# One input block beside each group of routing weights, 24 routed slots in that stage, weights read back for eight blocks at a time

## The chip, the cores and the metric

The kernel runs on one core of a Trainium2 chip. The metric is device time in microseconds, from launch to the last output; the times shown are medians over a few executions, and one execution was also recorded by the hardware profiler.

## The reference

One layer of a diffusion backbone over 512 tokens of width 1024. An adaLN, a mixer made of three head groups and an output projection come first; the change leaves them alone. Then comes an expert layer (PEER) with 16384 experts, of which each token uses 128:

```
q = (t @ w_q).reshape(n_tok, PEER_HEADS, 2, PEER_QDIM // 2)
s = einsum('thid,hikd->thik', q, sub_keys)      # 8 heads, 2 halves, 128 keys
v1, i1 = top_k(s[:, :, 0], 16);  v2, i2 = top_k(s[:, :, 1], 16)
top_s, pos = top_k(v1[..., :, None] + v2[..., None, :], 16)   # 16 experts a head
idx = i1 * 128 + i2 at pos;  g = softmax(top_s)               # 128 experts a token
act = gelu(einsum('tkd,td->tk', u_tab[idx], t))
out = einsum('tk,tkd->td', g * act, v_tab[idx])
return rmsnorm(h + g2 * out, final_g)
```

## The kernel before

**Two ways through the expert layer.** The tokens are four tiles of 128. Tiles 0 to 2 (384 tokens) go densely: the 16384 experts are 128 blocks of 128. For each block `a` TensorE multiplies the block of `u_tab` with the tokens (`u_block`: 24 matmuls with 384 columns, three for each of 8 chunks, because every fp32 operand is split into a high and a low part, `wh` and `wl`; the text calls it a U block). ScalarE applies GELU, the result is multiplied by the block's routing weights (`e_w`), split again (`wwh`, `wwl`), and multiplied with the block of `v_tab` (`e_v`: 18 matmuls of 512 columns, three into each of six PSUM accumulators; a V block). Tile 3 (128 tokens) goes by gathers, one of its 128 routed slots `k` after the other: `g_load` gathers one row of 8 KB for each token (POOL), `g_dot` forms the dot product (VectorE, DVE), `g_act` applies GELU and the gate (ScalarE, ACT: `actG`, `wG`), `g_acc` adds to `accG` (DVE).

**Stages.** After scores and top-k comes `weights_T`, which turns the routing into a dense table of weights. It runs over 3 tiles of 16 steps `q8`, here 48 groups. In a group DVE builds two one-hot operands (`oi`, `ow`), TensorE multiplies them (16 small matmuls into `gdps`, which take the high part of `ow` first and the low part second), and ACT copies the result out in two pieces (`stg`). Each four groups fill one `stg`, which is written to DRAM (`gd_d`, 2 MB). Blocks of the list `AHEAD` are taken through `u_block` and GELU early and their result is kept in DRAM (`act_d`): the generator `ahead_steps` does one of them at each `next(ahead)`. In `weights_T` that is in the groups of `UQ`, 12 of each 16. A slot of tile 3 is spread over four groups there: `g_acc(k - 1)`, `g_load(k + 3)` and `g_dot(k)` in the first, `g_act(k)` in the second.

**The loop over blocks.** Then the loop `for i in range(-6, P + 1)` takes the 128 blocks: V block `i`, the U block of `i + 2` unless it is in `AHEAD` (then `act_d` is read back as `acl`), and the slots `kG[i]` to `kG[i + 1]` of tile 3. The loads run on SP's queue in the order in which the loop calls `e_load` and `e_weights`; a load waits there for a free buffer, and what stands behind it on SP waits too.

The order of the instructions on each engine is that of the code (`manual_schedule`); every engine works its list in order.

Of the kernel before, what the change touches and what calls it, by code (L numbers as in the profile page):

```python
# [7 lines left out]
F32 = mybir.dt.float32  # L8
# [4 lines left out]
AF = mybir.ActivationFunctionType  # L13
ALU = mybir.AluOpType
# [3 lines left out]
P = 128  # L18
D = 1024
# [4 lines left out]
NX = SEQ // P  # L24
# [8 lines left out]
TQ = 32  # L33
NQ = TD // TQ
# [109 lines left out]
    "cst": (P, NCST), "pcnt": (P, 4 * SEQ),  # L144
}

NAHEAD = 74
AHEAD = [a for a in range(128) if a * NAHEAD % 128 < NAHEAD]


def build(tc, A, out, dbg=None):
# [1370 lines left out]
    def g_load(k):  # L1522
        if k < P:
            rows[k] = gt.tile([P, 2 * D], F32, name="row")
            G.indirect_dma_start(out=rows[k], out_offset=None, in_=A["peer_uv"],  # L1525
                                 in_offset=bass.IndirectOffsetOnAxis(ap=idxG[:, k:k + 1], axis=0))
# [9 lines left out]
    def g_acc(k):  # L1536
        row = rows.pop(k)
        if k:
            V.scalar_tensor_tensor(accG, row[:, D:2 * D], wG[:, k:k + 1], accG, ALU.mult, ALU.add)  # L1539
        else:  # L1540
            V.tensor_scalar(accG, row[:, D:2 * D], wG[:, k:k + 1], None, ALU.mult)
# [14 lines left out]
        V.scalar_tensor_tensor(gwT[:, qs, 1, :], by8(2), GSCALE, gwT[:, qs, 0, :], ALU.mult, ALU.subtract)  # L1556

    gq = {}

    def weights_T(t):  # L1560
        for q8 in range(16):
            if q8 % 4 == 0:
                stg = sg.tile([P, P, TQ], F32, name="stg")

            def tb(ap):
                return ap[:, t * 16 + q8].rearrange("p w (g c) -> p (w g) c", c=2).unsqueeze(2).broadcast_to([P, 8, P, 2])
            oi = gs2.tile([P, 2, 4, P, 2], F16, name="oi", bufs=3)
            V.tensor_tensor(oi.rearrange("p w g b c -> p (w g) b c"), iotaA.unsqueeze(1).broadcast_to([P, 8, P, 2]), tb(ixT), ALU.is_equal)
            ob, oa = oi[:, 0], oi[:, 1]
            ow = gs2.tile([P, 2, 4, P, 2], F16, name="ow", bufs=3)  # L1570
            for w in range(2):
                V.tensor_tensor(ow[:, w], oa, tb(gwT)[:, w * 4:w * 4 + 4], ALU.mult)
            oh, ol = ow[:, 0], ow[:, 1]
            for q4 in range(2):
                ps = psD.tile([P, 4, P], F32, name="gdps")
                for j in range(4):
                    tt = q4 * 4 + j
                    pr, c = tt // 2, tt % 2
                    PE.matmul(ps[:, j, :], ob[:, pr, :, c], oh[:, pr, :, c], start=True, stop=False)
                    PE.matmul(ps[:, j, :], ob[:, pr, :, c], ol[:, pr, :, c], start=False, stop=True)  # L1580
                t0 = q8 % 4 * 8 + q4 * 4
                S.activation(stg[:, :, t0:t0 + 4].rearrange("p a t -> p t a"), ps, AF.Copy, scale=1.0 / GSCALE)  # L1582
            if q8 % 4 == 3:
                (nc.gpsimd if t == 2 and q8 == 15 else nc.scalar).dma_start(gd_d[t * 4 + q8 // 4], stg)
            if q8 in UQ:
                next(ahead, None)
            k = t * 4 + q8 // 4
            gq[0] = stg
            if q8 % 4 == 0:
                if k:  # L1590
                    g_acc(k - 1)
                    g_load(k + 3)
                g_dot(k)
            elif q8 % 4 == 1:
                g_act(k)

    UQ = (0, 1, 3, 4, 5, 7, 8, 9, 11, 12, 13, 15)

    def whole(gen):
        for _ in gen:  # L1600
# [26 lines left out]
    psD = gdp.ps("psD", bufs=4)  # L1627
    for t in range(3):
        weights_T(t)
    g_acc(11)  # L1630
    g_load(15)
    whole(ahead)


# [4 lines left out]
    esp = Pools()  # L1639
    ex = esp.sb("ex", bufs=2)  # L1640
    glp = Pools()
    gl = glp.sb("gl", bufs=3)
    gls = [gl]
    psV = ep.ps("psV", bufs=1)
    accT = [[psV.tile([P, 512], F32, name=f"pv{t}{hf}") for hf in range(2)] for t in range(3)]
# [20 lines left out]

    def e_weights(a):

        if a % 4 == 0:
            n = NQ if a else NQ - 1  # L1670
            gd = gds[a // 4] = gls[a // 4 % 2].tile([P, NQ, 4 * TQ], F32, name="gd", bufs=1)
            nc.sync.dma_start(gd[:, 0:n, :], gd_d[0:n, :, a:a + 4, :].rearrange("q b a t -> b q (a t)"))
            if n < NQ:
                G.tensor_copy(gd[:, n, :], gq[0][:, 0:4, :].rearrange("p a t -> p (a t)"))

    def e_u(a):
        if a in AHEAD:
# [5 lines left out]
    def e_w(a):  # L1683

        x = ac.pop(a)
        xq = x.rearrange("p (q t) -> p q t", q=NQ)
        V.tensor_tensor(xq, xq, gds[a // 4][:, :, a % 4 * TQ:(a % 4 + 1) * TQ], ALU.mult)  # L1687
        wh = ex.tile([P, TD], F32R, name="wwh", bufs=3)
        wl = ex.tile([P, TD], F32R, name="wwl", bufs=3)
        lows[a, 2] = []  # L1690
        split(wh, wl, x, None, lows[a, 2])
        ww[a] = (wh, wl)
# [8 lines left out]
    def f_load():  # L1701

        nc.sync.dma_start(fgr, A["rowg"][:, D:2 * D])
        for t in (3, 0, 1, 2):
            nc.sync.dma_start(hx[:, t, :], h_d[t * P:(t + 1) * P, :])
        row_bc(g2r, psu, 2, 2)

    def f_mul(t, hf):

        if hf == 0:  # L1710
            sqs[t] = gt.tile([P, 2 * D], F32, name="row")
            fss[t] = e1.tile([P, 2], F32, name="fss", bufs=2)
        sq = sqs[t]
        hs = slice(hf * 512, (hf + 1) * 512)
        src = accT[t][hf] if t < 3 else accG[:, hs]
        if "peer" in dbg:
            V.tensor_copy(sq[:, hs], src)
            nc.sync.dma_start(dbg["peer"][t * P:(t + 1) * P, hs], sq[:, hs])
        V.tensor_tensor(sq[:, hs], src, g2r[:, hs], ALU.mult)
        (V if t == 2 else G).tensor_tensor(hx[:, t, hs], sq[:, hs], hx[:, t, hs], ALU.add)  # L1720

    def f_sq(t, hf):
        hs = slice(hf * 512, (hf + 1) * 512)
        S.activation(sqs[t][:, hs], hx[:, t, hs], AF.Square, accum_out=fss[t][:, hf:hf + 1])

    def f_rstd(t):
        V.tensor_tensor(fss[t][:, 0:1], fss[t][:, 0:1], fss[t][:, 1:2], ALU.add)
# [1 line left out]

    def f_gain(t, hf):  # L1730
        hs = slice(hf * 512, (hf + 1) * 512)
        (V if t == 2 else G).tensor_tensor(sqs[t][:, D + hf * 512:D + hf * 512 + 512], hx[:, t, hs], fgr[:, hs], ALU.mult)

    def f_norm(t):
        r = f_rstd(t)
# [11 lines left out]
    def within(f, i):  # L1747
        if 0 <= i < P:
            f(i)
    LAST = 3  # L1750
    kG = [12 + min(P - 12, (i * (P - 12) + 120) // 121) for i in range(P + 1)]
    with order:
        e_weights(0)
        sgp.close()
        gls.append(glp.sb("gl2"))
        e1 = ep.sb("e1", side="right")
        g2r = e1.tile([P, D], F32, name="g2r")
        fgr = e1.tile([P, D], F32, name="fgr")
        hx = e1.tile([P, NX, D], F32, name="hx")
        for i in range(-6, P + 1):  # L1760
            within(lambda a: e_load(a, 0), i + 6)
            within(lambda a: e_load(a, 1), i + 4)
            if i > -5:
                within(e_weights, i + 5)
            now = range(kG[i], kG[i + 1]) if 0 <= i < P else ()
            within(e_w, i + 1)
            for k in now:
                g_dot(k)
            within(lambda a: e_high(a, 0), i + 3)
            within(lambda a: e_high(a, 1), i + 1)  # L1770
            within(lambda a: e_low(a, 2), i + 1)
            within(lambda a: e_low(a, 0), i + 3)
            within(lambda a: e_low(a, 1), i + 1)
            for k in now:
                g_act(k)
            within(e_u, i + 2)
            for k in now:
                g_acc(k)
                g_load(k + 4)
            if 0 <= i < P - LAST:  # L1780
                for t in range(3):
                    e_v(i, t)
                del ww[i]
            if i == 64:
                f_load()
            if i == P - 4:
                f_mul(3, 0)
                f_mul(3, 1)
            if i == P - 3:
                f_sq(3, 0)  # L1790
                f_sq(3, 1)
                f_gain(3, 0)
                f_gain(3, 1)
            if i == P - 1:
# [50 lines left out]
```

## Time and profile before

| | before |
|---|---|
| median of 3 executions | 1920.64 us (1919.88 to 1920.69) |
| the profiled execution, its own time | 1921.22 us |
| its span, first to last instruction | 1919.5 us |
| TensorE (PE) busy | 1833.6 us, 96% |
| VectorE (DVE) busy | 1397.4 us, 73% |
| ScalarE (ACT) busy | 829.5 us, 43% |
| GpSimd (POOL) busy | 413.8 us, 22% |
| mean granted TensorE clock | 0.986 |

A record of a matmul runs from its start to a modelled end, and neighbours overlap; rates are read from start to start. In a row of the timeline, the bracket at the end gives the idle time just ahead of the instruction and what ended it.

### The profile page before, as it was taken

The numbers are of one execution on the slowest core, as the hardware profiler recorded it, in microseconds if no ns is written. First come the engines' busy times: TensorE is split into PE (matmuls) and PEld (weight loads), VectorE is DVE, ScalarE is ACT, GpSimd is POOL, SyncE is SP. The second block draws the span as 40 slices with busy tenths as digits, with TensorE's granted clock in tenths as the row PEclk, the third lists the DMA queues.
The fourth block names the chain that finished last, engine by engine and source line by source line (L and its number), as shares of the span: only waits on it lengthen the run. The fifth ranks groups of instructions, "written<-read, shape, count | busy, mean of one in ns | idle before, by whom it ended". The sixth has DMA issues, their size and how long they took to land.

```text
span 1919.5 us, 26340 instructions
## 1 busy us (share of the span) xinstructions
PE 1833.6 (96%) x9703; PEld 1543.0 (80%) x9703; DVE 1397.4 (73%) x2682; ACT 829.5 (43%) x1491; POOL 413.8 (22%) x309
## 2 busy tenths in 40 slices
PE   6999998878999899999899999999999999999997
PEld 4687776655777788999888988888888888888886
DVE  5553149996642458988788878878878778878875
ACT  4332224414643433345666754434444444444443
POOL 1102226572002554330001011111111111111103
PEclk9999999988999999999999999999999999999999
DMA  9546231216422443356578779998999998999971
GB/s 357 163 140 200 79 131 55 67 39 226 143 66 77 134 139 109 113 176 247 213 288 303 289 290 392 351 365 324 351 353 328 374 384 321 366 339 333 367 254 65
DMA packets 210194, 446.75 MB, mean 233 GB/s; under 512 B 13424, under 2 KB 137072, under 8 KB 192112
## 3 DMA queue, kind: packets, MB, share of 16 engines
q1 hardware_dynamic: 172192, 259.25, 40.4%
q0 software_dynamic: 18576, 136.32, 18.2%
q10 hardware_dynamic: 19296, 49.49, 7.1%
q8 instruction: 76, 1.25, 0.3%
q14 instruction: 54, 0.44, 0.1%
HBM read 394.81 MB, written 52.30 MB: 233 GB/s over the span
## 4 chain that ended last, share of the span: by engine, by line
PE 78%; DVE 11%; ACT 6%; issue 3%; DMA 1%; ACTq 0%; POOL 0%; SPq 0%; DVEq 0%; POOLq 0%
PE pv L188 9%; PE pv L187 9%; PE pv L189 9%; PE pu L187 8%; PE pu L189 8%; PE pu L188 8%; PE acc L187 4%; PE acc L188 4%; PE acc L189 4%; ACT stg L1582 2%; PE acc L419 1%; DVE wl L180 1%; PE acc L421 1%; PE po L1049 1%; PE acc L423 1%
## 5 line engine op out<-in xcount | busy, mean ns | idle before, releaser
L180 DVE TENSOR_TENSOR wl<-wraw,wh 128x1024 fp32r<-128x1024 f32 x290 | 357.3, 1248 | 164.5 <-ACT wh L177 160.6
L177 ACT ACTIVATE wh<-wraw 128x1024 fp32r<-128x1024 f32 x324 | 335.9, 1052 | 223.7 <-PE acc L188 75.1
L187 PE MATMUL pu<-u2h,wh 128*128 128x384 f32 (+2 forms) x1040 | 355.1, 341 | 0.2 <-ACT g2r L1093 0.2
L189 PE MATMUL pu<-u2h,wl 128*128 128x384 f32 (+2 forms) x1040 | 351.0, 338 | 2.5 <-DVE wl L180 2.5
L188 PE MATMUL pu<-u2l,wh 128*128 128x384 f32 (+2 forms) x1040 | 350.9, 337 | 0.0
L1525 POOL DMA_INDIRECT row<-in_peer_uv,idxG x128 | 134.6, 1051 | 849.0 <-DVE accG L1539 742.9
L188 PE MATMUL pv<-wl,wwh 128*128 128x512 f32 x768 | 303.2, 395 | 0.0
L187 PE MATMUL pv<-wh,wwh 128*128 128x512 f32 x768 | 303.1, 395 | 0.0
L189 PE MATMUL pv<-wh,wwl 128*128 128x512 f32 x768 | 303.1, 395 | 0.0
L187 PEld LDWEIGHTS pu<-u2h,wh 128*128 128x128 f32 x1040 | 197.1, 189 | 3.4 <-ACT g2r L1093 1.0
L189 PEld LDWEIGHTS pu<-u2h,wl 128*128 128x128 f32 x1040 | 196.9, 189 | 2.9 <-DVE wl L180 2.9
L188 PEld LDWEIGHTS pu<-u2l,wh 128*128 128x128 f32 x1040 | 196.9, 189 | 2.3
L189 PEld LDWEIGHTS pv<-wh,wwl 128*128 128x128 f32 x768 | 144.4, 188 | 34.4
L188 PEld LDWEIGHTS pv<-wl,wwh 128*128 128x128 f32 x768 | 144.4, 188 | 32.1 <-DVE wl L180 0.2
L187 PEld LDWEIGHTS pv<-wh,wwh 128*128 128x128 f32 x768 | 144.3, 188 | 32.1
L1539 DVE SCALAR_TENSOR_TENSOR accG<-row,wG,accG 128x1024 f32<-128x1024 f32 x127 | 162.4, 1279 | 0.0
L1530 DVE CUSTOM_DVE_ANT_0 row<-row,u2G 128x1024 f32<-128x1024 f32 x128 | 156.0, 1219 | 0.0
L1687 DVE TENSOR_TENSOR act<-act,gd 128x384 f32<-128x384 f32 x54 | 31.3, 579 | 131.3 <-ACT act L1681 130.5
L177 ACT ACTIVATE wwh<-acl 128x384 fp32r<-128x384 f32 x74 | 38.9, 526 | 191.7 <-DVE acl L1687 169.0
L1681 ACT ACTIVATE act<-pu 128x384 f32<-128x384 f32 x54 | 26.5, 491 | 207.3 <-PE pu L189 207.3
L1582 ACT ACTIVATE stg<-gdps 128x512 f32<-128x512 f32 x96 | 98.1, 1163 | 26.0 <-PE gdps L1580 21.6
L180 POOL TENSOR_TENSOR wl<-wraw,wh 128x1024 fp32r<-128x1024 f32 x34 | 81.7, 2404 | 113.2 <-ACT wh L177 94.7
(412 smaller groups left out, 3249.7 us busy)
## 6 DMA issues: line engine op xcount, KB each, us to landing
wraw<-in_peer_ut SPq DMA_DIRECT2D x128, 512.0 KB
wraw<-in_peer_uv SPq DMA_DIRECT2D x128, 512.0 KB
gd<-gd_d SPq DMA_DIRECT2D x31, 768.0 KB
gd_d<-stg ACTq DMA_DIRECT2D x11, 2048.0 KB
wraw<-in_w_in SPq DMA_DIRECT2D x36, 512.0 KB
acl<-act_d SPq DMA_DIRECT2D x74, 192.0 KB
act_d<-act ACTq DMA_DIRECT2D x72, 192.0 KB
kT<-in_ada_w SPq DMA_DIRECT2D x18, 512.0 KB
```

Of the source, the lines that this page charges most:

```text
L177: S.activation(hi, full, AF.Copy)
L180: (eng or V).tensor_tensor(lo, full, hi.bitcast(F32), ALU.subtract)
L187: PE.matmul(ps, ah, bh, start=start, stop=False)
L188: PE.matmul(ps, ah, bl, start=False, stop=False)
L189: PE.matmul(ps, al, bh, start=False, stop=stop)
L419: PE.matmul(px, h[:, k, :], uh[:, k, :], start=s, stop=False)
L1525: G.indirect_dma_start(out=rows[k], out_offset=None, in_=A["peer_uv"], in_offset=bass.IndirectOffsetOnAxis(ap=idxG[:, k:k + 1], axis=0))
L1530: V.tensor_tensor_reduce(row[:, 0:D], row[:, 0:D], u2G, 1.0, 0.0, ALU.mult, ALU.add, actG[:, k:k + 1])
L1539: V.scalar_tensor_tensor(accG, row[:, D:2 * D], wG[:, k:k + 1], accG, ALU.mult, ALU.add)
L1582: S.activation(stg[:, :, t0:t0 + 4].rearrange("p a t -> p t a"), ps, AF.Copy, scale=1.0 / GSCALE)
L1681: S.activation(ac[a], pu[:, :TD], AF.Gelu)
L1687: V.tensor_tensor(xq, xq, gds[a // 4][:, :, a % 4 * TQ:(a % 4 + 1) * TQ], ALU.mult)
```

## The change

It does six things. `NAHEAD` goes from 74 to 86, so 86 blocks are in `AHEAD` and 42 are not. Each of the 48 groups of `weights_T` gets a `next(ahead)`, where 36 had one. A slot of tile 3 is spread over two groups and not four (`k = t * 8 + q8 // 2`), so 24 slots stand there and not 12; `g_act` stands in every odd group. In the loop, the weights are read back for eight blocks in one load (four for the first and the last), one iteration earlier, and `acl` has four buffers for three. The slots that are left are dealt to the iterations in proportion to 1 for an iteration without and 2 for one with a U block. The residual rows `hx` are loaded at `i == P - 6` and not at `i == 64`, into a buffer of the weights and into `u2G`.

```diff
-NAHEAD = 74
+NAHEAD = 86
 def weights_T(t):
...
-            if q8 in UQ:
-                next(ahead, None)
-            k = t * 4 + q8 // 4
+            next(ahead, None)
+            k = t * 8 + q8 // 2
             gq[0] = stg
-            if q8 % 4 == 0:
+            if q8 % 2 == 0:
                 if k:
                     g_acc(k - 1)
                     g_load(k + 3)
                 g_dot(k)
-            elif q8 % 4 == 1:
+            else:
                 g_act(k)
-    UQ = (0, 1, 3, 4, 5, 7, 8, 9, 11, 12, 13, 15)
...
-    g_acc(11)
-    g_load(15)
+    g_acc(NMID - 1)
+    g_load(NMID + 3)
     whole(ahead)
...
-    gl = glp.sb("gl", bufs=3)
+    gl = glp.sb("gl", bufs=4)
...
     def e_weights(a):
-        if a % 4 == 0:
+        if a % 8 == 4 or a == 0:
+            m = 8 if 0 < a < P - 4 else 4
...
-            nc.sync.dma_start(gd[:, 0:n, :], gd_d[0:n, :, a:a + 4, :].rearrange("q b a t -> b q (a t)"))
+            nc.sync.dma_start(gd[:, 0:n, :], gd_d[0:n, :, a:a + m, :].rearrange("q b a t -> b q (a t)"))
...
-    kG = [12 + min(P - 12, (i * (P - 12) + 120) // 121) for i in range(P + 1)]
+    done = [sum(1 if a + 2 in AHEAD else 2 for a in range(i)) for i in range(P + 1)]
+    kG = [NMID + min(P - NMID, -(-done[i] * (P - NMID) // done[P - 8])) for i in range(P + 1)]
...
-                within(e_weights, i + 5)
+                within(e_weights, i + 6)
...
             if i == 64:
                 f_load()
+            if i == P - 6:
+                h_load()
```

The order on DVE in the middle of `weights_T`, one slot of tile 3 with the groups around it. `wl` is the low part of a U block to come, the two ISA rows are `g_dot`, `oi` and `ow` belong to a group of routing weights. Before, over four groups:

```order
L180 TENSOR_TENSOR wl<-wraw,wh 128x1024 [waits DMAHW5_49,Activation_49]
L1539 SCALAR_TENSOR_TENSOR accG<-row,wG,accG 128x1024
L1530 ISA row,actG<-row,u2G 128x1024 [waits DMASW2_49]
L1530 ISA actG 128x1
L1568 TENSOR_TENSOR oi<-iotaA,ixT 128x2048 [waits PE_49]
L1572 TENSOR_TENSOR ow<-oi,gwT 128x1024 [waits DVE_49]
L1572 TENSOR_TENSOR ow<-oi,gwT 128x1024
```

Of the change, over two groups:

```order
L180 TENSOR_TENSOR wl<-wraw,wh 128x1024 [waits DMAHW5_49,PE_49,Activation_49]
L1539 SCALAR_TENSOR_TENSOR accG<-row,wG,accG 128x1024 [waits Activation_49]
L1530 ISA row,actG<-row,u2G 128x1024 [waits DMASW3_49]
L1530 ISA actG 128x1
L1569 TENSOR_TENSOR oi<-iotaA,ixT 128x2048 [waits PE_49]
L1573 TENSOR_TENSOR ow<-oi,gwT 128x1024 [waits DVE_49]
L1573 TENSOR_TENSOR ow<-oi,gwT 128x1024
```

The instructions and their order are the same here; `accG` now carries a wait of its own for ACT, which the wait of `wl` ahead of it covered before.

The order on ACT in the same place. `act` is the GELU of a U block, `actG` and `wG` are `g_act`, `stg` are the copies of the routing weights. Before:

```order
L1303 ACTIVATE act_8384<-pu 128x384 [waits DMAHW6_49,PE_49]
L1304 DMA act_d<-act_8384 128x384 [waits Activation_49]
L1533 ACTIVATE actG<-actG 128x1 [waits DVE_49]
L1534 ACTIVATE wG<-actG,gG 128x1 [waits Activation_49]
L1582 ACTIVATE stg<-gdps 128x4x128 [waits PE_49] x4
L1584 DMA gd_d<-stg 128x4096 [waits Activation_49]
L177 ACTIVATE wh<-wraw 128x1024
L1303 ACTIVATE act_8471<-pu 128x384 [waits DMAHW0_49,PE_49]
```

Of the change:

```order
L1303 ACTIVATE act_8424<-pu 128x384 [waits DMAHW0_49,PE_49]
L1304 DMA act_d<-act_8424 128x384 [waits Activation_49]
L1533 ACTIVATE actG<-actG 128x1 [waits DVE_49]
L1534 ACTIVATE wG<-actG,gG 128x1 [waits Activation_49]
L1583 ACTIVATE stg<-gdps 128x4x128 [waits PE_49] x2
L177 ACTIVATE wh<-wraw 128x1024
L1303 ACTIVATE act_8485<-pu 128x384 [waits DMAHW2_49,PE_49]
```

Between `wG` and the next GELU there were four copies and a write; now there are two copies, and the GELU of the U block that was added.

The order on SP where the loop over blocks begins: `gd` are the weights read back, `acl` is a U block's kept result, `in_peer_ut` and `in_peer_uv` are blocks of `u_tab` and `v_tab`. Before:

```order
L208 DMA wraw<-in_peer_uv 128x1024 [waits Activation_49]
L208 DMA wraw<-in_peer_ut 128x1024 [waits DMAHW5_49,Activation_49]
L208 DMA wraw<-in_peer_uv 128x1024 [waits DMAHW6_49,DVE_49]
L1672 DMA gd<-gd_d 128x12x128 [waits DMASW7_49,DMAHW0_49,Activation_49,Pool_49]
L1651 DMA acl<-act_d 128x384 [waits DMAHW1_49,DVE_49]
```

Of the change:

```order
L208 DMA wraw<-in_peer_ut 128x1024 [waits DMAHW3_49,DMAHW2_49,Activation_49]
L208 DMA wraw<-in_peer_uv 128x1024 [waits DMAHW4_49,Activation_49]
L1674 DMA gd<-gd_d 128x12x256 [waits DMASW3_49,DMAHW6_49,Activation_49,Pool_49]
L1649 DMA acl<-act_d 128x384 [waits DMAHW7_49]
L208 DMA wraw<-in_peer_uv 128x1024 [waits DMAHW0_49]
```

The second read of the weights, which waits for the last piece written by POOL, is twice as large, and the load of V block 3 now stands behind it.

## Rows read from the trace of the kernel before

**Rows 1.** Busy time of each engine by stretches of the span (PE, PEld, DVE, ACT, POOL, each with its count of instructions), then the granted TensorE clock, the share of the DMA engines and GB/s. `weights_T` lies in 915 to 1137, the loop in 1137 to 1905.

```profile
950.00:1000.00 50.00, 45.91 (x362) 43.80 (x362) 42.04 (x49) 35.70 (x45) 5.03 (x3) 1.00 0.81 296
...
1050.00:1100.00 50.00, 45.92 (x377) 43.64 (x376) 42.54 (x50) 34.31 (x44) 3.59 (x3) 1.00 0.77 283
...
1150.00:1900.00 750.00, 749.85 (x3527) 647.24 (x3526) 605.38 (x779) 309.13 (x595) 115.19 (x116) 1.00 0.91 335
```

**Rows 2.** Who waited for whom from 900 to 1140 us: engine, what waited, what ended the wait, us in total, times, longest.

```profile
DVE wl L180 <- ACT wh L177: 35.0, 14, 4.4
...
PE gdps L1579 <- DVE ow L1572: 13.8, 12, 3.4
...
PE gdps L1580 <- DVE ow L1572: 4.4, 12, 0.4
```

**Rows 3.** The same from 1140 to 1900 us; the second and third row are the only ones of PE's sort.

```profile
ACT wwh L177 <- DMA gd<-gd_d: 8.3, 3, 2.8
...
PEld pu L187 <- ACT g2r L1093: 1.0, 1, 1.0
...
PE pu L187 <- ACT g2r L1093: 0.2, 1, 0.2
```

**Rows 4.** ACT's timeline in the middle of `weights_T`: start, duration, instruction.

```profile
1057.28 0.49 ACT L1303 ACTIVATE act<-pu 128x384 f32<-128x384 f32 x1 [1.80 <-PE pu L189]
1057.80 0.33 ACTq L1304 DMA_DIRECT2D act_d<-act  x1
1058.17 0.20 ACT L1533 ACTIVATE actG<-actG 128x1 f32<-128x1 f32 x1 [0.40 <-DVE ow L1572]
1058.40 0.29 ACT L1534 ACTIVATE wG<-actG,gG 128x1 f32<-128x1 f32 x1
1058.61 3.98 ACT L1582 ACTIVATE stg<-gdps 128x512 f32<-128x512 f32 x4
1062.62 0.33 ACTq L1584 DMA_DIRECT2D gd_d<-stg  x1
1062.99 1.06 ACT L177 ACTIVATE wh<-wraw 128x1024 fp32r<-128x1024 f32 x1 [0.40 <-ACT stg L1582]
...
1064.83 2.11 ACT L1582 ACTIVATE stg<-gdps 128x512 f32<-128x512 f32 x2 [0.40 <-ACT act L1303]
1066.72 1.08 ACT L177 ACTIVATE wh<-wraw 128x1024 fp32r<-128x1024 f32 x1
...
1075.50 0.49 ACT L1303 ACTIVATE act<-pu 128x384 f32<-128x384 f32 x1 [1.78 <-PE pu L189]
```

**Rows 5.** DVE's timeline in the same place.

```profile
1064.08 1.23 DVE L180 TENSOR_TENSOR wl<-wraw,wh 128x1024 fp32r<-128x1024 f32 x1 [2.52 <-ACT wh L177]
1065.23 1.28 DVE L1539 SCALAR_TENSOR_TENSOR accG<-row,wG,accG 128x1024 f32<-128x1024 f32 x1
1066.42 1.22 DVE L1530 CUSTOM_DVE_ANT_0 row<-row,u2G 128x1024 f32<-128x1024 f32 x1
...
1067.57 1.22 DVE L1568 TENSOR_TENSOR oi<-iotaA,ixT 128x2048 f16<-128x2048 f16 x1
1068.82 1.30 DVE L1572 TENSOR_TENSOR ow<-oi,gwT 128x1024 f16<-128x1024 f16 x2
1070.03 1.22 DVE L180 TENSOR_TENSOR wl<-wraw,wh 128x1024 fp32r<-128x1024 f32 x1
1071.16 1.22 DVE L1568 TENSOR_TENSOR oi<-iotaA,ixT 128x2048 f16<-128x2048 f16 x1
```

**Rows 6.** PE's timeline in the same place: the first matmul of a group of weights, the wait in the next group, and the first matmul of the U blocks and of the group behind.

```profile
1063.20 0.23 PE L1579 MATMUL gdps<-ow,oi 128*128 128x128 f16 x1
...
1064.10 0.42 PE L187 MATMUL pu<-u2h,wh 128*128 128x384 f32 x1
...
1069.57 0.23 PE L1579 MATMUL gdps<-ow,oi 128*128 128x128 f16 x1 [1.00 <-DVE ow L1572]
1070.17 0.22 PE L1580 MATMUL gdps<-ow,oi 128*128 128x128 f16 x1 [0.37 <-DVE ow L1572]
...
1071.00 0.42 PE L187 MATMUL pu<-u2h,wh 128*128 128x384 f32 x1
...
1075.31 0.24 PE L1579 MATMUL gdps<-ow,oi 128*128 128x128 f16 x1
```

**Rows 7.** PE's timeline in the loop: the first matmul of three V blocks, of a U block behind them, and of the V block behind that.

```profile
1505.75 0.40 PE L187 MATMUL pv<-wh,wwh 128*128 128x512 f32 x1
...
1518.35 0.34 PE L187 MATMUL pu<-u2h,wh 128*128 128x384 f32 x1
...
1522.58 0.40 PE L187 MATMUL pv<-wh,wwh 128*128 128x512 f32 x1
```

**Rows 8.** Both ends of `weights_T`: ACT's GELU of the second group's U block, and PE's first matmul of the last group's.

```profile
930.31 0.49 ACT L1303 ACTIVATE act<-pu 128x384 f32<-128x384 f32 x1 [1.35 <-PE pu L189]
...
1131.78 0.42 PE L187 MATMUL pu<-u2h,wh 128*128 128x384 f32 x1
```

**Rows 9.** The queues of POOL (first row) and SP where the loop begins.

```profile
1135.75 0.58 POOL L1584 DMA_DIRECT2D gd_d<-stg  x1 [12.64 <-ACT stg L1582]
...
1135.75 0.38 SPq L208 DMA_DIRECT2D wraw<-in_peer_uv  x1
1149.35 0.38 SPq L1672 DMA_DIRECT2D gd<-gd_d  x1
```

More of the change, by code (lines that the diff above doesn't have):

```diff
@@ L1558, in build @@
     gq = {}
+    NMID = 24
     def weights_T(t):
@@ L1667, in e_weights @@
     def e_weights(a):
-        if a % 4 == 0:
+        if a % 8 == 4 or a == 0:
+            m = 8 if 0 < a < P - 4 else 4
             n = NQ if a else NQ - 1
-            gd = gds[a // 4] = gls[a // 4 % 2].tile([P, NQ, 4 * TQ], F32, name="gd", bufs=1)
-            nc.sync.dma_start(gd[:, 0:n, :], gd_d[0:n, :, a:a + 4, :].rearrange("q b a t -> b q (a t)"))
+            if m == 4:
+                gd = gls[0].tile([P, NQ, 4 * TQ], F32, name="gd4", bufs=1)
+            else:
+                gd = gls[1].tile([P, NQ, 8 * TQ], F32, name="gd", bufs=2)
+            nc.sync.dma_start(gd[:, 0:n, :], gd_d[0:n, :, a:a + m, :].rearrange("q b a t -> b q (a t)"))
             if n < NQ:
                 G.tensor_copy(gd[:, n, :], gq[0][:, 0:4, :].rearrange("p a t -> p (a t)"))
+            for j in range(m):
+                gds[a + j] = gd[:, :, j * TQ:(j + 1) * TQ]
     def e_u(a):
@@ L1686, in e_w @@
         xq = x.rearrange("p (q t) -> p q t", q=NQ)
-        V.tensor_tensor(xq, xq, gds[a // 4][:, :, a % 4 * TQ:(a % 4 + 1) * TQ], ALU.mult)
+        V.tensor_tensor(xq, xq, gds.pop(a), ALU.mult)
         wh = ex.tile([P, TD], F32R, name="wwh", bufs=3)
@@ L1703, in f_load, with h_load @@
         nc.sync.dma_start(fgr, A["rowg"][:, D:2 * D])
+        row_bc(g2r, psu, 2, 2)
+    hx = {}
+    def h_load():
+        hr = gls[1].tile([P, NQ, 8 * TQ], F32, name="gd", bufs=2).rearrange("p q t -> p (q t)")
         for t in (3, 0, 1, 2):
-            nc.sync.dma_start(hx[:, t, :], h_d[t * P:(t + 1) * P, :])
-        row_bc(g2r, psu, 2, 2)
+            hx[t] = u2G if t == 3 else hr[:, t * D:(t + 1) * D]
+            nc.sync.dma_start(hx[t], h_d[t * P:(t + 1) * P, :])
     def f_mul(t, hf):
@@ L1719, in f_mul @@
         V.tensor_tensor(sq[:, hs], src, g2r[:, hs], ALU.mult)
-        (V if t == 2 else G).tensor_tensor(hx[:, t, hs], sq[:, hs], hx[:, t, hs], ALU.add)
+        (V if t == 2 else G).tensor_tensor(hx[t][:, hs], sq[:, hs], hx[t][:, hs], ALU.add)
     def f_sq(t, hf):
         hs = slice(hf * 512, (hf + 1) * 512)
-        S.activation(sqs[t][:, hs], hx[:, t, hs], AF.Square, accum_out=fss[t][:, hf:hf + 1])
+        S.activation(sqs[t][:, hs], hx[t][:, hs], AF.Square, accum_out=fss[t][:, hf:hf + 1])
     def f_rstd(t):
@@ L1731, in f_gain @@
         hs = slice(hf * 512, (hf + 1) * 512)
-        (V if t == 2 else G).tensor_tensor(sqs[t][:, D + hf * 512:D + hf * 512 + 512], hx[:, t, hs], fgr[:, hs], ALU.mult)
+        (V if t == 2 else G).tensor_tensor(sqs[t][:, D + hf * 512:D + hf * 512 + 512], hx[t][:, hs], fgr[:, hs], ALU.mult)
     def f_norm(t):
@@ L1758, in build @@
         fgr = e1.tile([P, D], F32, name="fgr")
-        hx = e1.tile([P, NX, D], F32, name="hx")
         for i in range(-6, P + 1):
```

## The prediction

> **What bounds the kernel now.** I read the busy times by stretches first [rows 1]. The loop keeps PE busy for 749.85 of 750 us, and the waits of that stretch hold nothing on PE above 1.0 us [rows 3]: there a matmul taken away is time taken away. `weights_T` is another regime: PE is busy 45.9 of 50 us, DVE 42, ACT 34 to 36, at the full clock (1.00, 2.4 GHz) and a DMA share near 0.8. None of them is full, so a chain through several engines sets the pace. The waits name its joints [rows 2]: DVE's `wl` waits for ACT's `wh` (35.0 us in 14 waits), and PE's group matmuls wait for DVE's `ow`, 12 times for the high part (13.8 us) and 12 times for the low part (4.4 us). Twelve is the number of slots of tile 3 there.
>
> The timelines let the chain be walked once around, four groups long. On ACT [rows 4] a GELU starts at 1057.28; 0.89 later, behind the issue of its write, comes `actG`, 0.23 later `wG`, 0.21 later four copies of 4.01, the issue of 0.37, then `wh`, whose end lets DVE's `wl` start 1.09 after it. On DVE [rows 5] `wl` to `accG` is 1.15, to the dot product 1.19, to `oi` 1.15, to `ow` 1.25, and 1.35 later PE's second matmul starts, which needs the low part [rows 6]. From there 0.83 to the U block (1071.00) and 4.50 to its GELU at 1075.50 [rows 4]. The turn is 18.22 us, and no link in it waits for anything outside it. DVE has 2.52 us and PE 1.37 us of idle time in that turn, ACT the rest.
>
> **The change part by part.**
>
> *The loop.* A U block lasts from 1518.35 to 1522.58, 4.23 us [rows 7]. PE is dense, so twelve fewer give back 12 x 4.23 = 50.8 us.
>
> *PE in `weights_T`.* A group costs 0.90 for its small matmuls and 4.31 for a U block with the switch behind it [rows 6], 5.21 together. Were PE the pace there, two groups would take 10.42 us. DVE's work for two groups, from [rows 5], is 2 x (1.25 + 1.21) for `oi` and `ow`, 1.15 + 1.13 for two `wl`, 1.19 + 1.15 for the slot: 9.54 us, which fits. ACT needs at most 1.33 + 1.89 + 1.08 + 0.37, under 4.7 us of each 5.21 [rows 4]. Each engine alone would let it go.
>
> *The chain of a slot.* It doesn't, because of the place of `g_act`. Before, `wG` is formed in the second group and `accG` uses it in the fifth; the wait lies three groups back and costs nothing. Now `wG(k - 1)` stands in the odd group directly ahead of the even group whose `accG` needs it, and on ACT it stands behind the GELU of that odd group's U block. So the turn is: GELU to `wG` 0.89 + 0.23, `wG` itself 0.29 [rows 4], and a hop to DVE. The hop isn't shown for this pair; `wh`, which ends at 1064.05, lets `wl` start at 1064.08 [rows 4, 5], which is 0.03, and the longest step of this sort that ACT shows is the 0.40 in the brackets of [rows 4]. I take 0.03, as it is the same pair of engines: 1.44 us. Then `accG` to the dot product 1.19, to `oi` 1.15, to `ow` 1.25, to the low part's matmul 1.35, to the U block of the next odd group 0.83, to its GELU 4.50 [rows 4 to 6]. The sum is 11.71 us for two groups. What is late next: DVE finishes its 9.54 us and waits about 2.2 for `wG`, where it waited for `wh`; behind `accG` stand the dot product, `oi` and `ow`, and for `ow` waits PE, 1.3 us in each second group. Where PE's idle time was 12 times 1.5 us, it becomes 23 times 1.3.
>
> *Length of the stage.* The second group's GELU is at 930.31 [rows 8], and nothing ahead of it moves. The last group is 46 groups, 23 turns, later: its GELU comes at 930.31 + 23 x 11.71 = 1199.6 and its U block starts 4.50 earlier, at 1195.1. Before, it starts at 1131.78 [rows 8]. That is +63.4 us. With the hop at 0.40 it would be 23 x 0.37 = 8.5 us more. At the lower end, no hop at all gives 0.7 less.
>
> *From the last group to the loop.* `accG(23)` must wait for a GELU too, about 5.9 us after the last group's U block begins, and two `wl` stand behind it. They end about 9.5 after that start; the first U block of the loop's own begins at 4.31 + 4.23 = 8.5 with the earlier of the two (8.4), the first V block at 12.8. I put it at 0 and keep 1 us.
>
> *The weights read back.* The second read waits for POOL's piece, which takes 1149.35 - 1135.75 = 13.6 us from its issue [rows 9]. It is twice as large now and V block 3 is queued behind it. This is the second rival. Elsewhere in the loop it is hidden: PE waits for none of these loads [rows 3], and ACT's 8.3 us for `gd` reach no one.
>
> *Slots and residual rows.* Twelve fewer slots in the loop take DVE and DMA work out of a stretch where neither is waited for by PE [rows 1, 3]: 0. The bytes fall by twelve gathers of 1.05 MB and twelve times 0.33 MB (0.52 for the block less 0.20 for its kept result), 16.5 of 251 MB (335 GB/s x 750 us), while the time falls by 50.8: the rate stays at 336 GB/s. The residual rows, 2.1 MB, are moved from a busy stretch to the last six iterations, some 25 us before they are used; at 335 GB/s they need 6.3 us. 0, with PE's V blocks as the cover.
>
> *The sum.* 63.4 - 50.8 = +12.6 us. The profiled execution took 1921.2 for a span of 1919.5; with the change 1933.8. It lies 0.6 above the median, so the median becomes **1933.2 us**.
>
> **The rivals.**
>
> *PE sets the pace of `weights_T`* (ends on the other side). Then the last U block starts at 930.31 + 46 x 5.21 - 4.50 = 1165.5, only 33.7 later, and the kernel takes 1903.5 us. What speaks for it: every engine's own work fits into 10.42. What speaks against it: the turn before is made of the same links, and each of them starts as soon as the one ahead of it lets it, with engines idle beside it. It decides from a turn of 11.16 us downwards, where the stage grows by as much as the loop shrinks: 0.55 of the links would have to overlap. The Trainium skill, in "Perfetto Trace Analysis", section "Optimization Strategy", says that where the most contended engine changes between stretches, interleaving the stretches may help. By that rule U blocks laid into the gaps of this stage would give this rival's time; the trace agrees that PE has gaps there, and shows that they end with `ow`, which more U blocks don't make earlier.
>
> *Loads late where the loop begins.* If S is the start of the last group's U block, POOL's write goes out some 2 us earlier than now (two copies ahead of it, not four), the read at about S + 15.6. V block 3 starts at S + 29.6 when PE is dense and needs 2.3 us for its split. Between lie the read (1.57 MB), a kept result (0.20) and the block (0.52), with two gathers 4.4 MB, 13.1 us at 335 GB/s: 1.4 us late, and in time without the gathers. With a second load late as well I price it at 1 to 5 us: 1934 to 1938.
>
> *The change doesn't do what it says.* Were the turn near 11.16 us, 12 U blocks would change places and the time would stay at 1920 to 1922.
>
> **How the numbers follow.** The chain alone has 0.72, the chain with late loads 0.12, PE at its own pace 0.10, no change 0.06. Time: 1933. The range goes from 1928 (the chain with 0.2 us of its links overlapping, 23 x 0.2 = 4.6) to 1942 (the hop at 0.40); below it lie the cases of the other sign, 0.16. About 0.2%, 4 us, is what a measurement of this kernel can tell from no change: faster 0.10, same 0.06, slower 0.84.
>
> **What would show it.** Right: two groups of `weights_T` take 11.7 us; `accG` waits for ACT's `wG` some 23 times, about 2.2 us each; PE waits for `ow` in each odd group, about 1.3 us; the loop is dense on PE and about 50 us shorter. Wrong: no wait of `accG`, a turn of 10.4 us; or waits of PE for `wl` of blocks in the loop, or a granted clock below 1.00 in the stage.

## The result, and the profile after

| | before | after |
|---|---|---|
| median of 4 executions (range) | 1920.55 us (1919.88 to 1920.69) | 1935.18 us (1934.28 to 1935.73) |
| profiled execution: its time, its span | 1921.2, 1919.5 | 1934.28, 1932.4 |
| GELU of the second group's U block, in `weights_T` | 930.31 | 927.69 |
| GELU of the last group's U block | 1136.3 | 1197.08 |
| between the two | 206.0 | 269.4 |
| from there to the end of the span | 783.2 | 735.3 |

The ratio is 1.0076, 95% interval 1.0059 to 1.0094: 0.76% slower. (1136.3 is the matmul at 1131.78 in [rows 8] and the 4.50 us from a U block to its GELU.)

The busy times by stretches of the changed kernel, to be held against [rows 1]: `weights_T` lies in 915 to 1202, the loop behind it.

```profile
950.00:1150.00 200.00, 182.98 (x1366) 172.65 (x1365) 164.00 (x188) 125.92 (x170) 28.51 (x17) 1.00 0.85 300
1215.00:1912.00 697.00, 694.65 (x3216) 592.43 (x3214) 564.27 (x724) 286.68 (x543) 118.52 (x103) 1.00 0.90 335
```

PE is busy 45.7 of 50 us in the stage, hardly other than before, though there are a third more U blocks to fill it with: the stage became longer, not denser. The loop is shorter and nearly as dense as it was (694.65 of 697 us).

Who waited for whom from 900 to 1203 us, to be held against [rows 2].

```profile
DVE accG L1539 <- ACT wG L1534: 42.5, 23, 5.7
...
PE gdps L1580 <- DVE ow L1573: 17.5, 23, 3.5
DVE wl L180 <- ACT wh L177: 9.6, 12, 2.4
PE gdps L1581 <- DVE ow L1573: 8.8, 24, 0.4
```

The first row stands nowhere in the trace of before: `accG` waits for `wG` 23 times, once for each slot behind the first (the 5.7 is the last slot's, behind the last group). `wl` behind `wh`, the largest wait before, is down to about a quarter. PE still waits for `ow`, now 23 times.

One turn of that chain, first on ACT, then on DVE, then PE's waits in two turns; to be held against [rows 4 to 6].

```profile
1056.23 0.49 ACT L1303 ACTIVATE act<-pu 128x384 f32<-128x384 f32 x1 [1.17 <-PE pu L189]
1056.75 0.33 ACTq L1304 DMA_DIRECT2D act_d<-act  x1
1057.13 0.20 ACT L1533 ACTIVATE actG<-actG 128x1 f32<-128x1 f32 x1 [0.40 <-ACT act L1303]
1057.36 0.29 ACT L1534 ACTIVATE wG<-actG,gG 128x1 f32<-128x1 f32 x1
...
1067.96 0.49 ACT L1303 ACTIVATE act<-pu 128x384 f32<-128x384 f32 x1 [1.78 <-PE pu L189]
```

```profile
1055.10 1.23 DVE L180 TENSOR_TENSOR wl<-wraw,wh 128x1024 fp32r<-128x1024 f32 x1 [0.65 <-ACT wh L177]
...
1057.69 1.29 DVE L1539 SCALAR_TENSOR_TENSOR accG<-row,wG,accG 128x1024 f32<-128x1024 f32 x1 [1.36 <-ACT wG L1534]
1058.89 1.22 DVE L1530 CUSTOM_DVE_ANT_0 row<-row,u2G 128x1024 f32<-128x1024 f32 x1
...
1060.04 1.22 DVE L1569 TENSOR_TENSOR oi<-iotaA,ixT 128x2048 f16<-128x2048 f16 x1
1061.29 1.29 DVE L1573 TENSOR_TENSOR ow<-oi,gwT 128x1024 f16<-128x1024 f16 x2
...
1069.41 1.28 DVE L1539 SCALAR_TENSOR_TENSOR accG<-row,wG,accG 128x1024 f32<-128x1024 f32 x1 [1.97 <-ACT wG L1534]
```

```profile
1062.04 0.23 PE L1580 MATMUL gdps<-ow,oi 128*128 128x128 f16 x1 [0.64 <-DVE ow L1573]
1062.64 0.22 PE L1581 MATMUL gdps<-ow,oi 128*128 128x128 f16 x1 [0.37 <-DVE ow L1573]
```

From GELU to GELU, and from `accG` to `accG`, it is 11.73 and 11.72 us for two groups. `wG` ends at 1057.65 and `accG` starts at 1057.69: a hop of 0.04.

### The profile page after: what moved, and what is told of

Its sections match the earlier page's. It is cut to its first block, busy times and chain, and to the rows that moved or that the text cites. A ratio compares the mean times of both kernels' runs of the same rounds, so it can differ in the third digit from the quotient of the medians.

```text
span 1932.4 us, 26430 instructions
## 1 busy us (share of the span) xinstructions
PE 1837.3 (95%) x9703; PEld 1541.7 (80%) x9703; DVE 1405.1 (73%) x2682; ACT 833.6 (43%) x1491; POOL 440.6 (23%) x309
## 4 chain that ended last, share of the span: by engine, by line
PE 77%; DVE 12%; ACT 4%; issue 3%; DMA 2%; POOL 1%; ACTq 0%; SPq 0%; DVEq 0%; POOLq 0%
PE pv L188 9%; PE pv L189 9%; PE pv L187 9%; PE pu L187 7%; PE pu L189 7%; PE pu L188 7%; PE acc L187 4%; PE acc L188 4%; PE acc L189 4%; PE acc L419 2%; PE acc L421 1%; DVE accG L1539 1%; PE acc L423 1%; DVE oi L1569 1%; PE po L1049 1%
## 5 line engine op out<-in xcount | busy, mean ns | idle before, releaser
L1525 POOL DMA_INDIRECT row<-in_peer_uv,idxG x128 | 157.3, 1229 | 849.5 <-DVE accG L1539 750.2
L1530 DVE CUSTOM_DVE_ANT_0 row<-row,u2G 128x1024 f32<-128x1024 f32 x128 | 155.3, 1220 | 0.0
L177 ACT ACTIVATE wwh<-acl 128x384 fp32r<-128x384 f32 x86 | 45.2, 526 | 204.9 <-DVE acl L1691 142.8
L1685 ACT ACTIVATE act<-pu 128x384 f32<-128x384 f32 x42 | 20.6, 490 | 162.0 <-PE pu L189 162.0
L1303 ACT ACTIVATE act<-pu 128x384 f32<-128x384 f32 x84 | 41.0, 489 | 111.1 <-PE pu L189 106.7
```

The source lines that it names most:

```text
L177: S.activation(hi, full, AF.Copy)
L1303: S.activation(act, pu[:, :TD], AF.Gelu)
L1530: V.tensor_tensor_reduce(row[:, 0:D], row[:, 0:D], u2G, 1.0, 0.0, ALU.mult, ALU.add, actG[:, k:k + 1])
L1685: S.activation(ac[a], pu[:, :TD], AF.Gelu)
```

## The experiments

The theory is the chain of the prediction: each slot is a closed round of GELU, `wG`, `accG`, dot product, `oi`, `ow`, PE, U block, 11.7 us for two groups, whatever each engine could do alone. The rivals are that 48 U blocks are too many for the stage in themselves, that the loop's new parts cost the time, and that the waits only show slack while something else sets the pace. Diffs are against the changed kernel unless something else is said. Before had 1922.0, 1920.7 and 1920.9 us as its median beside the three batches of runs; each ratio is against the one of its own batch.

**One link shorter: `wG` ahead of the GELU.** In odd groups `g_act` stands ahead of the piece of the U blocks, so that `wG` no longer waits for that group's GELU.

```diff
-            next(ahead, None)
             k = t * 8 + q8 // 2
+            if q8 % 2:
+                g_act(k)
+            next(ahead, None)
...
-            else:
-                g_act(k)
```

> The change with one thing moved on ACT: in an odd group g_act stands ahead of the U block's split and GELU instead of behind them, so that wG no longer waits for TensorE. Nothing is added or left out. Chain theory: the turn through wG is gone; the next longest is GELU, two copies, actG and wG, write issue, wh, then wl, accG, dot, oi, ow, U block and the U block behind it: 21.3 us for four groups (10.65 for two) where the change takes 23.4. That is 11.5 x 2.1 = 24 us less: about 1911 us (1905 to 1914), no wait of accG for wG. Rival (the sheer work of 48 U blocks and 24 slots in the stage sets its length): nothing of the work changes, so 1935 within 3 us.

Measured: 1915.71 us (1914.03 to 1916.01), ratio 0.9968 [0.9956, 0.9981]. One order on ACT turns the change from slower to faster than before. Its waits from 915 to 1185 us:

```profile
DVE wl L180 <- ACT wh L177: 29.5, 24, 2.9
...
PE gdps L1581 <- DVE ow L1573: 4.4, 12, 0.4
...
DVE accG L1539 <- ACT wG L1534: 2.7, 1, 2.7
```

Of the 23 waits of `accG` for `wG` one is left, that of the last slot, behind the last group. The stage takes 247.3 us between the same two GELUs, 10.75 for two groups. That is 0.33 over PE's own 10.42: by turns 11.44 and 10.09 from `accG` to `accG`, the longer one where `g_act` stands behind the copies and the write of a piece on ACT and `wl` waits for `wh`. I had reckoned with 10.65, so the stage missed by 0.1 a turn, some 2 us. The median lies 1.7 us above the upper end of what was expected. In the profiled execution the rest of the miss lies ahead of the stage, which begins 3.6 us later than in the changed kernel; behind the stage nothing differs (735.4 us against 735.3).

**One link taken out: `accG` in the odd group.**

```diff
             if q8 % 2 == 0:
+                g_dot(k)
+            else:
                 if k:
                     g_acc(k - 1)
                     g_load(k + 3)
-                g_dot(k)
-            else:
                 g_act(k)
```

> The change with g_acc(k - 1) and g_load(k + 3) moved from the even to the odd group, so that accG uses a wG formed two groups earlier and stands apart from the dot product. Nothing is added or left out. Chain theory: no chain is longer than PE's own 5.21 us a group, two groups take 10.42 to 10.5, the stage is 23 x 1.29 = 29.7 us shorter than in the change: about 1905.5 us (1903 to 1910), faster than the kernel before. Rival (the work sets the length): 1935 within 3 us.

Measured: 1913.87 us (1911.59 to 1917.46), ratio 0.9965 [0.9950, 0.9979]. The stage does what the theory says: 241.2 us, 10.49 for two groups, PE's own pace within 0.07, and PE has no gap in the middle of it. The median is 8 us above the expected time, and above the 1910 at which the range ended. In the profiled execution (1911.59, the fastest of five) 1.5 us of the miss lie in the stage and 5.9 behind it, at the entry of the loop, where PE loses only 0.8 us in the changed kernel (busy times by stretches, then PE's waits):

```profile
1050.00:1100.00 50.00, 50.00 (x379) 48.48 (x378) 45.50 (x54) 35.62 (x49) 8.36 (x5) 1.00 0.94 355
...
1180.00:1200.00 20.00, 14.93 (x67) 12.28 (x66) 11.35 (x15) 5.15 (x10) 2.05 (x2) 0.90 1.03 399
1200.00:1220.00 20.00, 20.00 (x87) 16.87 (x87) 17.88 (x24) 8.60 (x16) 5.27 (x4) 0.93 0.94 348
```

```profile
1198.28 0.80 PE L187 MATMUL pv<-wh,wwh 128*128 128x512 f32 x1 [4.60 <-ACT wh L177]
1199.54 0.79 PE L188 MATMUL pv<-wl,wwh 128*128 128x512 f32 x1 [0.46 <-DVE wl L180]
```

The split of a V block is late where the loop begins, since ACT waits for the block's load:

```profile
1197.17 1.06 ACT L177 ACTIVATE wh<-wraw 128x1024 fp32r<-128x1024 f32 x1 [8.57 <-DMA wraw<-in_peer_uv]
```

The granted clock falls around the gap (0.90 and 0.93 in the two stretches), so that the matmuls behind the gap take 0.80 where they take 0.40 in [rows 7]. From the last group's GELU to the end this kernel needs 741.2 us where the changed one needs 735.3.

**The slots alone.** 24 slots over two groups each, but 36 U blocks in the stage as before.

```diff
-NAHEAD = 86
+NAHEAD = 74
...
+    UQ = (0, 1, 3, 4, 5, 7, 8, 9, 11, 12, 13, 15)
...
-            next(ahead, None)
+            if q8 in UQ:
+                next(ahead, None)
```

> The change with 74 blocks ahead again: 36 U blocks in the 48 groups as before, but 24 slots, g_act in each odd group. Nothing is added or left out. Chain theory: the turn through wG goes through the U blocks of groups 1 and 3 and is as long as in the change, 23.4 us for four groups, where the kernel before takes 18.2, with no U block fewer in the loop: 1920.6 + 11.5 x 5.2 = 1980 us (1972 to 1984). Rival (PE or DVE work sets the stage's length): PE has the work of before and DVE 17.9 us for four groups, so 1921 within 4 us.

Measured: 2008.43 us (2006.89 to 2011.47), ratio 1.0451 [1.0434, 1.0469]. So the slots are the part of the change that costs, and more than I expected. Waiting matmuls of two turns, then two stretches of 50 us:

```profile
1039.91 0.29 PE L1581 MATMUL gdps<-ow,oi 128*128 128x128 f16 x1 [4.90 <-DVE ow L1574]
...
1053.25 0.23 PE L1581 MATMUL gdps<-ow,oi 128*128 128x128 f16 x1 [0.64 <-DVE ow L1574]
...
1064.98 0.29 PE L1581 MATMUL gdps<-ow,oi 128*128 128x128 f16 x1 [4.91 <-DVE ow L1574]
```

```profile
1000.00:1050.00 50.00, 37.56 (x268) 35.38 (x267) 35.02 (x42) 25.24 (x36) 6.04 (x4) 0.86 0.72 250
1050.00:1100.00 50.00, 37.55 (x267) 35.36 (x267) 35.06 (x42) 25.11 (x35) 6.71 (x4) 0.86 0.71 249
```

Where a pair of groups holds two U blocks the turn is 11.73 us, exactly as in the changed kernel; where it holds one, PE has a gap of 4.9 us in place of the block, the clock behind the gap is below full (matmuls of the U block at 1042 us start every 0.32 us, from 1044 on every 0.17 to 0.18), and the turn takes 12.6 to 14.4. I had expected 11.7 there too, hence 1980 and not 2008. The stage is 294.5 us long, 25.1 more than with 48 U blocks; the rest of the kernel takes 782.5, as before. So the change has two large parts of opposite sign: the slots cost 294.5 - 206.0 = 88.5 us in the stage, and the twelve U blocks, beside these slots, give back 25.1 in the stage and 47.2 in the loop.

**The loop's parts alone.** The stage of before, with the reads of eight blocks, the fourth buffer of `acl`, the new spread of the slots and the late residual rows.

```diff
-NAHEAD = 86
+NAHEAD = 74
...
-    NMID = 24
+    NMID = 12
```

(with the lines of `weights_T` as before)

> The kernel before with the loop's parts of the change alone: weights read back for eight blocks one iteration earlier, four acl buffers, slots dealt by PE time, residual rows loaded last; weights_T and the 74 blocks as before. Nothing is added or left out. My theory: PE is dense in the loop, so these parts are worth nothing but the small waits seen at the loop's two ends in the change (0.8 and 1.6 us): 1920 to 1923 us. Rival (longer reads relieve the DMA queues and the loop gets shorter): 1915 or less.

Measured: 1920.59 us (1916.68 to 1923.18), ratio 0.9997 [0.9987, 1.0007]. These parts are free, as costed.

**The U blocks alone.** 48 U blocks, but twelve slots over four groups each, so that `wG` is again three groups ahead of its `accG`.

```diff
-    NMID = 24
+    NMID = 12
...
-            k = t * 8 + q8 // 2
+            k = t * 4 + q8 // 4
...
-            if q8 % 2 == 0:
+            if q8 % 4 == 0:
...
-            else:
+            elif q8 % 4 == 1:
```

> The change with 48 U blocks kept in weights_T but 12 slots there, each spread over four groups again, so that wG is formed three groups ahead of its accG. If the place of the slots made the loss, no accG waits for wG, a group takes 5.2 to 5.3 us on PE, the last GELU of the stage comes at about 1168 to 1172 and the kernel takes 1904 to 1909; with V block 3 late at the entry of the loop, as in the kernel with g_acc moved, up to 1914. If 48 U blocks are too many for the stage in themselves: 1930 or more.

Measured: 1909.13 us (1908.41 to 1911.33), ratio 0.9944 [0.9930, 0.9959]. Busy times by stretches:

```profile
950.00:1000.00 50.00, 49.73 (x386) 48.07 (x384) 39.55 (x45) 34.73 (x45) 3.35 (x2) 1.00 0.79 265
...
1180.00:1200.00 20.00, 19.25 (x89) 16.05 (x88) 15.71 (x21) 8.06 (x17) 2.90 (x3) 1.00 1.03 399
```

PE is dense, the stage takes 242.4 us, 10.54 for two groups. That 48 U blocks are too many is refuted. Twelve more of them are 12 x 4.23 = 50.8 us of PE's work and lengthen the stage by 242.4 - 206.0 = 36.4: the 14 us between are gaps of PE that they fill. The loop is shorter by 47.3 (735.9 us from the last GELU to the end). Beside the packed slots the same twelve made the stage 25.1 us shorter, so the two parts don't simply add up: what a U block costs in the stage depends on whether the chain is there.

**A dose on the chain.** `wG` is formed three times in a row in the stage's slots, with the same value.

```diff
     def g_act(k):
         S.activation(actG[:, k:k + 1], actG[:, k:k + 1], AF.Gelu)
-        S.activation(wG[:, k:k + 1], actG[:, k:k + 1], AF.Copy, scale=gG[:, k:k + 1])
+        for _ in range(3 if k < NMID - 1 else 1):
+            S.activation(wG[:, k:k + 1], actG[:, k:k + 1], AF.Copy, scale=gG[:, k:k + 1])
```

> The change, with wG formed three times in a row in the slots of weights_T (the same value, so two more small ACT instructions in each link from GELU to accG; from start to start such a step takes 0.20 to 0.29 us in the traces). If the chain GELU, wG, accG, dot, oi, ow, U block sets the pace of the stage, every extra tenth on it comes back in each of 23 turns: 23 x 0.40 to 0.58 = 9 to 13 us, 1944 to 1949 in all, the turn 12.1 to 12.3 and not 11.72. If PE, DVE or the transfers set the pace and the waits for wG are only a place where slack shows, ACT's idle time takes it up: 1934 to 1937.

Measured: 1960.03 us (1957.93 to 1964.49), ratio 1.0215 [1.0200, 1.0229]. ACT's rows for it, then DVE's, then two stretches of 6 us, one turn apart:

```profile
1067.11 0.20 ACT L1533 ACTIVATE actG<-actG 128x1 f32<-128x1 f32 x1 [0.40 <-ACT act L1303]
1067.35 0.95 ACT L1535 ACTIVATE wG<-actG,gG 128x1 f32<-128x1 f32 x3
```

```profile
1055.94 1.28 DVE L1540 SCALAR_TENSOR_TENSOR accG<-row,wG,accG 128x1024 f32<-128x1024 f32 x1 [2.64 <-ACT wG L1535]
...
1068.33 1.28 DVE L1540 SCALAR_TENSOR_TENSOR accG<-row,wG,accG 128x1024 f32<-128x1024 f32 x1 [2.00 <-ACT wG L1535]
...
1082.26 1.29 DVE L1540 SCALAR_TENSOR_TENSOR accG<-row,wG,accG 128x1024 f32<-128x1024 f32 x1 [4.24 <-ACT wG L1535]
```

```profile
1059.00:1065.00 6.00, 4.35 (x35) 4.23 (x36) 5.36 (x7) 3.60 (x4) 0.16 (x1) 1.00 0.85 294
...
1071.00:1077.00 6.00, 4.35 (x29) 3.90 (x28) 5.93 (x8) 3.53 (x5) 0.56 (x1) 0.79 1.01 364
```

The three take 0.95 where one took 0.29: 0.66 more. From `accG` to `accG` it is 12.39, 0.66 to 0.67 more. The chain passes the dose on one to one, though ACT is idle a third of that time, so nothing beside it sets the pace. The expectation was short for two reasons: a repeat costs 0.33 and not 0.20 to 0.29 (23 dosed turns lie between the two GELUs that bound the stage, 23 x 0.66 = 15.2 us), and in five of the turns the granted clock falls (0.79 above) and they take 13.92 to 14.19: 7.9 us more. Together 23.1; the stage grew by 22.9.

**The late V block in the kernel with `accG` in the odd group.** First the order in SP's queue: the read-back one iteration later, so that V block 3 stands ahead of it, and the residual rows two iterations earlier (against that kernel).

```diff
-                within(e_weights, i + 6)
+                within(e_weights, i + 5)
...
-            if i == P - 6:
+            if i == P - 8:
```

> The kernel with g_acc in the odd groups (1913.9), with the weights read back one iteration later (i + 5, as before the change), so that V block 3 stands ahead of the large read in SP's queue, and with the residual rows two iterations earlier. In that kernel PE waited 4.6 + 0.5 us for V block 3's split at 1193 to 1199 and ran below full clock from 1180 to 1220 (granted 0.90 and 0.93, some 3 us). If the order in SP's queue made that loss: no wait of PE over 1 us at the entry, clock 1.00, 1905 to 1909. If V block 3 is late because the DMA engines are full in any case: the wait moves to it or to a block next to it, 1912 to 1915.

Measured: 1914.14 us (1911.88 to 1917.30), ratio 0.9968 [0.9956, 0.9980]: nothing won. The wait has gone to the next V block:

```profile
1206.78 0.68 PE L187 MATMUL pv<-wh,wwh 128*128 128x512 f32 x1 [4.17 <-ACT wh L177]
```

So the order decides which block is late, and not that one is. Then the bytes: no slot in the loop's first seven iterations (against the kernel with `accG` in the odd group).

```diff
-    kG = [NMID + min(P - NMID, -(-done[i] * (P - NMID) // done[P - 8])) for i in range(P + 1)]
+    kG = [NMID + min(P - NMID, -(-max(0, done[i] - done[7]) * (P - NMID) // (done[P - 8] - done[7])))
+          for i in range(P + 1)]
```

> The kernel with g_acc in the odd groups (first measured at 1913.9, a ratio of 0.9965 to before), with no slot of tile 3 in the loop's first seven iterations and the remaining slots dealt to those behind them. From 1150 to 1195 it and the kernel with 48 U blocks and 12 slots do the same loads, but two gathers of 1.05 MB more in it, 2.6 us each at 400 GB/s, and it alone waits 4 to 5 us on PE for a V block. If these bytes make the V block late: no wait of PE over 2 us there, no stretch below full clock, 1905 to 1909 (ratio 0.992 to 0.994). If the order in which the read-back and the loads stand behind POOL's piece makes it late whatever the bytes: a wait of 3 us or more again and 1912 to 1915.

Measured: 1907.61 us (1906.69 to 1908.83), ratio 0.9931 [0.9918, 0.9944], where the kernel with `accG` in the odd group had 0.9965 [0.9950, 0.9979]. The stretches from 1180 to 1220 us again:

```profile
1180.00:1200.00 20.00, 19.27 (x89) 16.08 (x89) 9.30 (x13) 7.82 (x11) 0.00 (x0) 1.00 1.04 396
1200.00:1220.00 20.00, 20.00 (x93) 16.94 (x92) 14.63 (x19) 8.68 (x13) 0.00 (x0) 1.00 0.89 312
```

PE's wait is down to 0.7 us, the clock is full, and from the last GELU to the end it takes 735.0 us instead of 741.2. With the slots postponed, their gathers leave the stretch, and the read-back and the loads fit. The slots' work on DVE and ACT leaves it too, and this run doesn't part the two; that it was the bytes rests on ACT's row in the kernel with `accG` in the odd group, where ACT was idle for 8.57 us and waited for the load.

> The kernel with 48 U blocks and 12 slots (1909.1, a ratio of 0.9944), with the same shift of the loop's first slots. There PE waits only 0.75 us at the entry, so little is to be had: 1907 to 1910 if the later, denser slots (104 in 113 iterations) cost nothing, 1911 or more if they make DVE or the DMA engines late for PE further on.

The same edit on the kernel with 48 U blocks and twelve slots: 1908.76 us (1906.10 to 1910.76), ratio 0.9935 [0.9923, 0.9947]. Beside 0.9944 [0.9930, 0.9959] no gain can be told, as expected where only 0.75 us were lost; the trace has no wait of PE at the entry any more.

## Why the prediction was right

- **The chain.** Predicted 11.71 us for two groups, measured 11.72 to 11.73; 23 turns grew the stage by 269.4 - 206.0 = 63.4, the number predicted. That it is a chain, and not one full engine, is shown by the two kernels that take a link away (10.75 and 10.49) and the one that adds 0.66 and gets 0.66 back.
- **The hop.** Taken as 0.03, measured 0.04. The other end, 0.40, would have given 1942.
- **Who waits.** `accG` waits for `wG` 23 times, as forecast: 1.36 and 1.97 us by turns, and 5.7 for the last slot. In the turn with the shorter one, `wl` waits 0.65 as well, so DVE idles about 2.0 us in each turn where 2.2 was forecast, all of it at `accG`. PE's waits for `ow` read 0.64 and 0.37, together 1.01, because they are counted from the modelled ends of the matmuls before them. From start to start a turn is 11.73 - 10.42 = 1.31 longer than PE's own work, which is the forecast 1.3.
- **The loop.** -50.8 was forecast; from the last group's GELU to the end it is 783.2 - 735.3 = 47.9 less. Of the 2.9 us that are missing, PE's waits from 1203 to 1913 show 2.4:

```profile
PE pv L188 <- DVE wl L180: 2.1, 3, 0.8
...
PE pv L187 <- ACT wh L177: 0.3, 1, 0.3
```

  0.76 of it is V block 3, late as the second rival had it (its `wh` waited 3.68 us for its load): the mechanism was there, below the 1 to 5 us I gave it. The rest, 1.6, lies at 1907 to 1912, in the last V blocks of the loop. A term for that end was missing. The kernel with the loop's parts alone has no wait of this kind there. With 86 blocks ahead, blocks 126 and 127 both come without a U block, with 74 only 127. All eight kernels here with 86 blocks ahead show these three waits, and neither of the two with 74 and the same loop does, so they go with the blocks taken out. That the shorter last iterations leave DVE too little time, while POOL's work on the residual rows slows it, is argued and not shown. The remaining 0.5 us is within the 1 us kept for the step from the last group to the loop.
- **The start.** I said that nothing moves ahead of the stage; its second GELU is 2.6 us earlier. This isn't the change: in the kernel with the stage of before and only the loop's parts new the same GELU comes at 932.2, 1.9 later than before, and over the kernels here it scatters from 927.3 to 932.7. The profiled executions differ by such amounts ahead of the stage.
- **The sum.** -2.6 + 63.4 - 47.9 = +12.9, the difference of the spans; +12.6 was forecast, on errors of 2.6 and 2.9 that cancel. The 63.4 came out of the chain as forecast; that the sum came within 0.3 us is in part luck. The median moved by 14.6, to 2.0 us above the forecast.
- **PE at its own pace.** The rival on the other side is what the stage can do: 1903.5 us was its price, and the kernels without the chain came to 1907.6 and 1909.1. What decided was the place of one instruction. By the Trainium skill ("Perfetto Trace Analysis", section "Optimization Strategy") interleaving stretches whose most contended engines differ may help. The kernel with 48 U blocks and twelve slots agrees (0.9944), and the changed kernel shows a limit (1.0076): where a chain through several engines sets the pace, the same U blocks in the same stage don't pay.
- **What I didn't see.** U blocks in the stage do more than fill gaps. Without the twelve, the gaps of 4.9 us cost clock, 25.1 us in all, so the change contained a larger loss and a larger gain than my two terms show. The sum wasn't touched, since in the changed kernel each of these gaps is filled by a U block and the clock stays at 1.00.

## What to carry to other kernels

Before work is moved into the gaps of a stage, walk its in-order loops once around. Look how far behind its producer each result's consumer stands: shortening that distance (here from three groups to one, with the producer behind a GELU) can make a closed chain out of a wait that cost nothing. At two groups, a whole turn, the chain was gone. Where every engine's own work fits and the stage still doesn't run at the pace of the fullest one, as here, look for the one instruction that can be moved across a neighbour (`accG` behind, or `wG` ahead of, a U block), then for the next limit (here the bytes at the loop's entry), which shows only once the first is gone. Two parts of opposite sign in one change are worth measuring apart: the U blocks alone won 0.6%, the slots alone lost 4.5%, and together they lost 0.8%.

## What the runs showed of the hardware

- The granted clock falls behind short gaps of PE, though not behind each. It is 1.00 in the changed kernel with 0.64 + 0.37 us idle in each turn, 0.86 in the stretches of the stage with a gap of 4.9 us in every second turn (a mean of parts at the 1.2 GHz and parts at the 2.4 GHz level, as the two rates of the U block's matmuls above show). With three `wG` it falls in five of 22 turns from `accG` to `accG`, with gaps of 1.28 to 1.30 us (once 1.57) and 0.37 us, and not in the others, which have the same gaps. What tells the turns apart stays open.
- A repeat of a one-column ACT instruction on the same column costs 0.33 us, against 0.21 from `wG` to the next instruction, which is independent of it [rows 4].
- At the loop's entry the DMA engines are at a share of 1.03 to 1.04 and deliver 396 to 399 GB/s; there two gathers of 1.05 MB more or less in the stretch went with a wait of PE of 4.6 or 0.7 us for a V block.
- Beside POOL's work on the residual rows, DVE's instructions with two inputs take 1.8 to 2.9 times as long. POOL's rows in the changed kernel, then DVE's product of an activation and its weights and a `wl`, ahead of them, beside them and behind them:

```profile
1901.60 3.25 POOL L1731 TENSOR_TENSOR u2G<-row,u2G 128x512 f32<-128x512 f32 x2 [54.45 <-DVE row L1730]
1904.80 3.84 POOL L1743 TENSOR_TENSOR row<-u2G,fgr 128x512 f32<-128x512 f32 x2
```

```profile
1897.59 0.56 DVE L1691 TENSOR_TENSOR act<-act,gd 128x384 f32<-128x384 f32 x1 [5.74 <-ACT act L1685]
...
1902.03 1.65 DVE L1691 TENSOR_TENSOR acl<-acl,gd 128x384 f32<-128x384 f32 x1
...
1905.28 2.23 DVE L180 TENSOR_TENSOR wl<-wraw,wh 128x1024 fp32r<-128x1024 f32 x1
...
1910.65 1.23 DVE L180 TENSOR_TENSOR wl<-wraw,wh 128x1024 fp32r<-128x1024 f32 x1 [0.39 <-ACT wh L177]
```

  With POOL idle the product takes 0.56 us and `wl` 1.23. The Trainium skill says in "SBUF — State Buffer", section "SBUF: two separate sides", that a VectorE instruction with two SBUF inputs and a GpSimd instruction that reads SBUF hold a shared pair of ports in turn, the later one blocked while the other runs. The trace agrees in direction: DVE's instructions are 1.0 to 1.1 us longer, where one of POOL's takes 1.6 to 1.9; no run here takes POOL's work away.
